# Tokens, memory tokens and norm weights laid out transposed by the host, with a tile shared in SBUF and other TensorE costs in a planner

## The chip, the cores and the metric

The kernel runs on one core of a Trainium2 chip. The metric is the device time of one execution in microseconds; three executions of the kernel before gave 803.38, 802.14 and 803.23 us, a median of 803.23 us. One further execution was recorded by the profiler, and every row below comes from it.

## What is computed

Two decoder layers over 256 tokens of width 1024 in float32. Each layer is a token mixer, a cross-attention into 256 memory tokens and a SwiGLU block, each behind an RMS norm and added to the residual stream `x`. Cut to what the change touches:

```python
h = rms_norm(x, norm_mix[i])            # x / sqrt(mean(x*x) + eps) * gain
if i % 2 == 0: x = x + dsa_moba_mixer(h, ...)      # token indexer, top 64 keys, two head groups
else:          x = x + nsa_mixer(h, ...)           # compressed, selected and window branches
q = rms_norm((rms_norm(x, norm_mem[i]) @ w_q), q_norm)
k, v = split(rms_norm(mem, norm_mem_src[i]) @ w_kv)
x = x + (softmax(q @ rms_norm(k, k_norm).T * scale) @ v) @ w_o
x = x + swiglu(rms_norm(x, norm_ffn[i]), w_in, w_out)
```

## The kernel before, in words

**Products.** Every float32 operand of a big product is split into a rounded half and a remainder (`hi`, `lo`), and each product is three matmuls (`mm3`): hi·hi, hi·lo, lo·hi. A product needs its tokens with the model dimension on the partitions. So the norm (`norm`, line 619) transposes `x` on TensorE, four 128x128 blocks per half row block, and `evac_gain` (line 608) multiplies by the norm's weights on DVE into `gv`, rounds that into the tile `h` (hi) and subtracts for the other half (lo). The scale 1/rms of a token is applied later, after the product, from sums of squares that ACT makes of the untransposed `x` (the tile `junk` takes the squares, accumulated into `ss`).

**Weights.** `plan_block` lists all weight blocks of 2x128x512 in the order of use. `load` (line 374) brings one by SP's queue into one of 3 buffers `raw`; `pusher` (line 395) makes its hi half (ACT or DVE) and its lo half (DVE) in one of 6 buffers `whl`, frees `raw` and issues the next load. `gemm` (line 571) walks the blocks for one tile of 128 tokens, 12 matmuls for a block of 512 columns; 1024 rows are four blocks.

**Order.** All work is written as generators. `Steps.run` (line 84) picks, one instruction at a time, the ready operation that an estimate of the engines' clocks (`Est`, line 140, with the costs of `cost`, line 236) lets start first. The order in which instructions stand on each engine is thus fixed when the program is built, from estimated costs; on the chip each engine takes its instructions in that order and waits with semaphores. Almost every instruction is recorded at one line (L232), so rows are told apart by tiles.

**Names.** In layer 0 the first product (`s`, 424 columns: `mm` with 128x424) feeds the small heads and the indexer; then follow `aq`, `bk`, `bq`, `bv`. `di`, `dk` and `t` are evacuated pieces that TensorE transposes (into `tp`), `ikT` the indexer's keys, `sp` scores, `acc` the indexer's sum, from which `top` (line 839) takes the best 64 keys, `sn` the softmax, `pt` its transpose, `po` the values' product. `mem_prep` (line 1242, spawned after `bq` in layer 0 and after the last query product in layer 1) loads the memory tokens (512 KB per 128 tokens), squares, transposes and splits them into buffers `slab`; `mem_k` (line 1267) then runs the product `mk`, which starts for a tile of 128 tokens when all 1024 dimensions of that tile are there. Line 448 on holds the start: the first loads of `x`, of the weights, and of `rows`, the norm weights as 76 rows of 128, which one TensorE transpose turns into `gT`.

Of the kernel before, what the change touches and what calls it, by code (L numbers as in the profile page):

```python
# [15 lines left out]
P = 128  # L16
D = 1024
# [122 lines left out]
class Est:  # L140


    def __init__(self, nc):
        self.clk = {"PE": 0.0, "V": 0.0, "S": 0.0, "G": 0.0, "D": 0.0, "port": 0.0}
        self.wr, self.rd, self.busy = {}, {}, {}
        self.now = 0.0
        self.eng = {n: Est.Engine(self, n, e) for n, e in
                    (("PE", nc.tensor), ("V", nc.vector), ("S", nc.scalar), ("G", nc.gpsimd))}
# [45 lines left out]
    def issue(self, e, outs, ins, cost):  # L194
        lock = self.locks(e, outs, ins)
        t = max(self.clk[e], self.after(e, outs, ins), self.clk["port"] if lock else 0.0)
        if e == "PE":
# [6 lines left out]
            cost = c  # L204
        t += cost
# [8 lines left out]
    class Engine:  # L214
# [21 lines left out]
        def cost(self, name, a, k, outs, ins):  # L236
# [58 lines left out]
def trunk(ctx: ExitStack, tc: tile.TileContext, I, out):  # L295
# [59 lines left out]

    def load_x(t, h, at):
# [91 lines left out]
    load_x(0, 0, 3.5)  # L448
    nc.sync.dma_start(rows, I["gains"])
    est.note(rows, est.wr, 3.6, "D")  # L450
    load_x(0, 1, 4.4)
    clk["D"] = 3.3
    load(0, 1.1)
    load(1, 1.1)
    for h in range(2):
        clk["D"] += 0.73
        load_x(1, h, clk["D"] + 1.1)
    for i in range(2, RAWS):
        load(i, 1.1)
# [9 lines left out]
    gps, f = TP.take([P, 512])  # L469
    T.transpose(gps[:, :NG], rows, ident[:NG, :NG]).issue()  # L470
    gT = cp.tile([P, NG], F32, name="gT")
    V.tensor_copy(gT, gps[:, :NG]).issue()
    f()
# [12 lines left out]
    def tables():  # L486
# [21 lines left out]
        yield has(("mix0", 0), 2)  # L508
# [62 lines left out]
    def gemm(key, t, h, K, ev, need=None, part=None):  # L571
# [15 lines left out]

    def both(key, h, K, ev):
# [5 lines left out]
    junk = tp.tile([P, 512], F32, name="junk")  # L594
# [24 lines left out]
    def norm(key, t, col, ver):  # L619
# [10 lines left out]
        ss = tiny(2, "ss")  # L630
        for h in range(2):
            yield S.activation(junk, x[t][:, 512 * h:512 * h + 512], AF.Square, accum_out=ss[:, h:h + 1])
        vr[key, t] = yield from ms_root(ss, "h", 0, t)

# [115 lines left out]
    def mixer0():  # L750
# [3 lines left out]
        ikT = hp.tile([P, SEQ], F32R, name="ikT")  # L754
        av = hp.tile([P, NT, HD], F32, name="av")
# [83 lines left out]
        def top(t, nk, acc):  # L839
# [5 lines left out]
            b = hp.tile([P, SEQ], F32, name=f"bias{t}")  # L845
# [99 lines left out]
        for t in range(NT):  # L945
            yield from gemm((0, "s"), t, h[t], KD, ev_small, (("mix0", t), 0))
# [26 lines left out]
    def mixer1():  # L973
# [4 lines left out]
        kvT = hp.tile([P, G + 1, SEQ], F32, name="kvT")  # L978
# [250 lines left out]
        for t in range(NT):  # L1229
            yield from gemm((1, "kc"), t, h[t], KD, ev_kc, (("mix1", t), 0))  # L1230
# [11 lines left out]
    def mem_prep(L):  # L1242
        m = I["mem"][0].rearrange("(t p) d -> t p d", p=P)
        for t in range(NT):
            raw, rf = yield from T4.get([P, D])
            nc.sync.dma_start(raw, m[t])
            est.note(raw, est.wr, clk["PE"] + 6.0, "D")
            ss = tiny(2, "mss")
            for h in range(2):
                rs = raw[:, 512 * h:512 * h + 512]  # L1250
                yield S.activation(junk, rs, AF.Square, accum_out=ss[:, h:h + 1])
                hi = yield from SL.get([P, 4, P], F32R)
                lo = yield from SL.get([P, 4, P], F32R)
                ps, f = yield from TP.get([P, 512])
                for k in range(4):
                    yield T.transpose(ps[:, k * P:(k + 1) * P], rs[:, k * P:(k + 1) * P], ident)
                col = 32 + 8 * L + 4 * h
                yield from evac_gain(ps, f, hi[0], lo[0], gT[:, col:col + 4])
                mT[t, h] = (hi, lo)
            rf()  # L1260
            mvr[t] = yield from ms_root(ss, "m", L, t)
            done(("mT", L, t))

    def msel(t):
        return lambda k: tuple(mT[t, k // 4][e][0][:, k % 4, :] for e in range(2))
# [271 lines left out]
```

## Time and profile before

| | us |
|---|---|
| median of three executions | 803.23 |
| the profiled execution | 801.81 |
| its span, first to last instruction | 800.1 |
| TensorE matmul busy (PE) | 766.0 |
| TensorE weight load busy (PEld) | 632.1 |
| VectorE busy (DVE) | 537.5 |
| ScalarE busy (ACT) | 435.4 |

Of the rest, GpSimd (POOL) is busy for 130.9 us, and the DMA queues move 121.27 MB. PE leads by far; what is not in its busy time are 34 us in which it waits. The columns of a stretch tell how busy each engine is in it, with the number of instructions in brackets, then the granted TensorE clock as a share of full speed, the mean busy share of the 16 DMA engines and what they moved. Behind a row's bracket "idle before" stands the time that the engine had waited and what ended the wait. PEld overlaps PE.

### The profile page before, as it was taken

What the parts mean: (1) busy time and instruction counts of PE and PEld (TensorE: products, weight loads), DVE (VectorE), ACT (ScalarE), POOL (GpSimd) and SP (SyncE); (2) the same over time, 40 slices, a digit from 0 to 9 for tenths busy, and PEclk for the clock granted to TensorE, in tenths of its full rate; (3) what the DMA queues carried; (4) which work ended last, traced back from release to release, by engine and by line L of the source; (5) the groups of instructions that cost most, each with busy time, mean ns of one, the idle gap of its engine ahead of it and who ended that gap; (6) DMA issues with size and microseconds to landing.
All of it is one profiled execution on the core that took longest, in us unless ns stands there. A gap on an engine that the chain in (4) does not pass through costs nothing.

```text
span 800.1 us, 11833 instructions
## 1 busy us (share of the span) xinstructions
PE 766.0 (96%) x4259; PEld 632.1 (79%) x4259; DVE 537.5 (67%) x1096; ACT 435.4 (54%) x816; POOL 130.9 (16%) x192
## 2 busy tenths in 40 slices
PE   6878999999999999999999988999999999999998
PEld 5766777888888888888878776878897888889886
DVE  6779998877655655545727798887868565646541
ACT  5666887565544434444526788864656334435430
POOL 1544332110000000000007463230200000000000
PEclk9999999999999999999999999999999999999999
DMA  7613334635565553887315632033635656546761
GB/s 221 208 55 112 134 124 122 181 119 159 158 191 179 168 186 119 240 251 224 116 56 148 210 112 81 1 103 110 184 105 146 198 184 180 167 141 209 225 184 52
DMA packets 69482, 121.27 MB, mean 152 GB/s; under 512 B 8420, under 2 KB 15664, under 8 KB 69424
## 3 DMA queue, kind: packets, MB, share of 16 engines
q1 hardware_dynamic: 69392, 120.53, 49.2%
q8 instruction: 33, 0.54, 0.3%
q14 instruction: 25, 0.20, 0.1%
q0 software_dynamic: 32, 0.00, 0.0%
HBM read 119.46 MB, written 1.05 MB: 151 GB/s over the span
## 4 chain that ended last, share of the span: by engine, by line
PE 83%; DVE 7%; ACT 4%; DMA 2%; issue 2%; POOL 1%; SPq 0%; POOLq 0%; ACTq 0%; DVEq 0%
PE mm L232 61%; PE po L232 12%; PE tp L232 7%; PE sp L232 3%; DVE whl L232 2%; DMA raw<-in_ab_w_in 1%; DMA raw<-in_ffn_w_in 1%; ACT sn L232 1%; ACT whl L232 1%; DVE slab L232 1%; DVE acc L232 1%; ACT slab L232 1%; DVE sn L232 1%; DVE t L232 1%; POOL sn L232 1%
## 5 line engine op out<-in xcount | busy, mean ns | idle before, releaser
L232 PE MATMUL mm<-whl,h 128*128 128x512 f32 (+3 forms) x1776 | 397.8, 379 | 8.5 <-DVE whl L232 6.9
L232 PEld LDWEIGHTS mm<-whl,h 128*128 128x128 f32 x1776 | 310.8, 189 | 68.0 <-DVE whl L232 8.9
L232 DVE TENSOR_TENSOR whl<-raw,whl 128x1024 fp32r<-128x1024 f32 (+3 forms) x232 | 270.9, 1170 | 116.6 <-ACT whl L232 112.4
L232 ACT ACTIVATE whl<-raw 128x1024 fp32r<-128x1024 f32 (+3 forms) x211 | 213.2, 1014 | 160.1 <-DMA raw<-in_ffn_w_in 38.4
L232 PE MATMUL mm<-whl,slab 128*128 128x512 f32 (+1 forms) x840 | 200.2, 376 | 0.9 <-DVE x L232 0.8
L232 PEld LDWEIGHTS mm<-whl,slab 128*128 128x128 f32 x840 | 140.6, 189 | 27.7 <-issue 2.4
L232 PE MATMUL po<-whl,slab 128*128 128x512 f32 x264 | 68.4, 396 | 0.0
L232 ACT ACTIVATE slab<-tp 128x256 fp32r<-128x256 f32 (+2 forms) x63 | 28.3, 471 | 56.3 <-PE tp L232 55.9
L232 PEld LDWEIGHTS po<-whl,slab 128*128 128x128 f32 x264 | 49.4, 188 | 11.4
L232 POOL TENSOR_TENSOR rh<-vh,mhalf 128x1 f32<-128x1 f32 x12 | 9.5, 794 | 293.6 <-DVE vh L232 283.1
L232 ACT ACTIVATE sn<-sn,mx 128x128 f32<-128x128 f32 (+1 forms) x96 | 42.7, 447 | 6.9 <-DVE mx L232 6.5
L232 PE MATMUL tp<-ident,t 128*128 128x128 f32 x224 | 34.8, 277 | 2.7 <-DVE slab L232 2.3
L232 PE MATMUL tp<-ident,sn 128*128 128x128 f32 (+1 forms) x180 | 30.9, 281 | 4.8 <-POOL sn L232 3.8
L232 DVE TENSOR_TENSOR x<-mm,x 128x512 f32<-128x512 f32 x36 | 24.6, 687 | 16.0 <-PE mm L232 15.9
L232 PEld LDWEIGHTS tp<-ident,t 128*128 128x128 f32 x224 | 27.1, 142 | 9.6 <-DVE slab L232 2.8
L232 ACT ACTIVATE pt<-tp 128x512 f32<-128x512 f32 (+2 forms) x51 | 27.0, 536 | 13.7 <-PE tp L232 11.8
L232 DVE CUSTOM_DVE_ANT_0 sn<-sp,cm,rq 128x128 f32<-128x128 f32 (+1 forms) x80 | 30.5, 410 | 4.9 <-PE sp L232 3.8
L232 POOL TENSOR_TENSOR sn<-sn,rc 128x512 f32<-128x512 f32 (+2 forms) x27 | 25.5, 944 | 43.5 <-DVE rc L232 28.6
L232 ACT ACTIVATE t<-mm,rh 128x512 f32<-128x512 f32 (+1 forms) x26 | 17.0, 654 | 27.0 <-PE mm L232 27.0
L232 PEld LDWEIGHTS tp<-ident,sn 128*128 128x128 f32 (+1 forms) x180 | 20.7, 141 | 11.6 <-POOL sn L232 5.2
L232 ACT ACTIVATE t<-mm 128x512 f32<-128x512 f32 (+2 forms) x46 | 23.7, 553 | 10.0 <-PE mm L232 8.0
L232 DVE SCALAR_TENSOR_TENSOR t<-mm,rh,t 128x512 f32<-128x512 f32 (+1 forms) x24 | 16.9, 704 | 18.2 <-PE mm L232 18.2
(200 smaller groups left out, 676.3 us busy)
## 6 DMA issues: line engine op xcount, KB each, us to landing
raw<-in_ffn_w_in SPq DMA_DIRECT2D x80, 512.0 KB, 3.8
raw<-in_ffn_w_out SPq DMA_DIRECT2D x44, 512.0 KB, 4.5
raw<-in_ab_w_in SPq DMA_DIRECT2D x16, 512.0 KB, 3.9
raw<-in_mem_w_kv SPq DMA_DIRECT2D x16, 512.0 KB, 4.0
raw<-in_nsa_w_in SPq DMA_DIRECT2D x16, 512.0 KB, 3.7
raw<-in_ab_w_out SPq DMA_DIRECT2D x8, 512.0 KB, 3.6
raw<-in_mem_w_q SPq DMA_DIRECT2D x8, 512.0 KB, 4.2
raw<-in_mem_w_o SPq DMA_DIRECT2D x8, 512.0 KB, 3.6
```

Source lines behind the costliest of these rows:

```text
L232: return f(*a, **{q: v() if q in ("start", "stop") and callable(v) else v for q, v in k.items()})
```

## The change

The host adds three arrays: `x_t` and `mem_t` (128 partitions x 8 x 256 tokens: the tokens transposed) and `gains_t` (128 x 76). `gT` is loaded and not transposed. For the first norm, four loads of 256 KB bring `x_t` into `slab` buffers, and `norm0` makes hi (rounded product with the weight of the partition) and lo from each 128x128 block; the rows of `x` are loaded behind them, for the sums of squares and the residual. `mem_prep` does the same with `mem_t`, two times 128 dimensions at a time for all 256 tokens, in both layers, and `mk` may begin with the first pair of dimensions. `mem_root` loads the rows of `mem` as well, in layer 0 alone, and its roots serve both layers. `junk` is gone (squares go to a free `t2` buffer), and the indexer's `acc` and `bias` live in a tile that layer 1's `kvT` takes over (`tag="kvT"`). In the planner, a switch between outputs of up to 64 partitions and more costs 0.09 us, a matmul at a column position 0.012 instead of 0.053, and a rounded one n x 0.00043 + 0.009 instead of n x 0.000422.

```diff
@@ Est.issue
+            thin = outs[0].shape[0] <= 64
+            if thin != self.thin:
+                t += 0.09
+            self.thin = thin
@@ Est.Engine.cost
                 if k.get("tile_position", (0, 0))[1]:
-                    return 0.053
+                    return 0.012
                 if ins[0].dtype == F32R:
-                    return n * (1 if n >= 256 else 4) * 0.000422
+                    return n * 0.00043 + 0.009
@@ trunk, the start
-    load_x(0, 0, 3.5)
+    nc.sync.dma_start(gT, I["gains_t"])
+    xfirst = []
+    for i in range(NB):
+        r, f = SL.take([P, 2, SEQ])
+        nc.sync.dma_start(r, I["x_t"][:, 2 * i:2 * i + 2])
...
+        xfirst.append((r, f))
+        if i < RAWS:
+            load(i, 1.1)
     nc.sync.dma_start(rows, I["gains"])
...
-    T.transpose(gps[:, :NG], rows, ident[:NG, :NG]).issue()
-    V.tensor_copy(gT, gps[:, :NG]).issue()
+    def gained(src, gain, hi, lo):
+        yield move(hi, src, gain)
+        yield V.scalar_tensor_tensor(lo, src, gain, hi.bitcast(F32), op0=OP.mult, op1=OP.subtract)
+    def norm0():
+        for b in range(NB):
+            r, f = xfirst[b]
+            for j in range(2):
+                k = 2 * b + j
+                for t in range(NT):
+                    yield from gained(r[:, j, t * P:(t + 1) * P], gT[:, k:k + 1], hT[t][0][:, k], hT[t][1][:, k])
+            f()
+            done("mix0")
...
@@ index
-                acc = hp.tile([P, SEQ], F32, name="acc", tag="acc", bufs=2)
+                acc = rowsT[:, t, :]
@@ mem_prep
-            raw, rf = yield from T4.get([P, D])
-            nc.sync.dma_start(raw, m[t])
+            raw, rf = yield from T2.get([P, 2, SEQ])
+            nc.sync.dma_start(raw, I["mem_t"][:, 2 * b:2 * b + 2])
...
-                for k in range(4):
-                    yield T.transpose(ps[:, k * P:(k + 1) * P], rs[:, k * P:(k + 1) * P], ident)
-                yield from evac_gain(ps, f, hi[0], lo[0], gT[:, col:col + 4])
+                yield from gained(raw[:, j], gT[:, c:c + 1], hi[0][:, j], lo[0][:, j])
...
-            yield has(("mT", L, t))
-            yield from gemm((L, "mk"), t, msel(t), KD, ev)
+            yield from gemm((L, "mk"), t, msel(t), KD, ev, pairs(("mT", L)))
```

Because the planner decides the order, work moves in both attention stretches. Three places:

SP's queue at the start of the program, before (`raw` are weight blocks):

```order
L358 DMA x_72<-in_x 128x512
L449 DMA rows<-in_gains 76x128
L358 DMA x_72<-in_x 128x512
L381 DMA raw_79<-in_ab_w_in 128x2x424
L381 DMA raw_81<-in_ab_w_in 128x2x424
L358 DMA x_73<-in_x 128x512 x2
L381 DMA raw_85<-in_ab_w_in 128x2x424
L381 DMA raw_159<-in_ab_w_in 128x2x424
```

and with the change:

```order
L457 DMA gT<-in_gains_t 128x76
L462 DMA slab_78<-in_x_t 128x512
L389 DMA raw_80<-in_ab_w_in 128x2x424
L462 DMA slab_82<-in_x_t 128x512
L389 DMA raw_84<-in_ab_w_in 128x2x424
L462 DMA slab_86<-in_x_t 128x512
L389 DMA raw_88<-in_ab_w_in 128x2x424
L462 DMA slab_90<-in_x_t 128x512
L468 DMA rows<-in_gains 76x128
L366 DMA x_72<-in_x 128x512 x2
L366 DMA x_73<-in_x 128x512 x2
L389 DMA raw_157<-in_ab_w_in 128x2x424
```

The first weight block moves ahead of half of the tokens, and the fourth now stands behind all of the transposed and all of the plain tokens.

TensorE in layer 0, before, at the end of the first tile of `bk` (`mm_444`), where the indexer's pieces are transposed and its scores made:

```order
L232 MATMUL mm_444<-whl_422,h_112 128x512
L232 MATMUL tp_509<-ident,di 128x128
L232 MATMUL tp_513<-ident,t_431 128x128 x4
L232 MATMUL tp_527<-ident,t_431 128x128 x4
L232 MATMUL tp_530<-ident,t_469 128x128 x4
L232 MATMUL sp_544<-ikT,slab_512 128x256 x2
L232 MATMUL tp_556<-ident,t_469 128x128 x4
L232 MATMUL sp_566<-ikT,slab_512 128x256 x2
L232 MATMUL tp_572<-ident,dk 128x128
L232 MATMUL sp_584<-ikT,slab_526 128x256 x2
L232 MATMUL tp_581<-identr,t_542 128x128 x4
L232 MATMUL tp_598<-identr,t_542 128x128 x2
```

and with the change, where the first of these stand in the two tiles of `aq` (`mm_361`, `mm_434`), one product earlier:

```order
L238 MATMUL mm_361<-whl_342,h_117 128x512 x2
L238 MATMUL mm_361<-whl_342,h_118 128x512
L238 MATMUL mm_361<-whl_342,h_117 128x512 x2
L238 MATMUL tp_425<-ident,t_330 128x128 x4
L238 MATMUL mm_361<-whl_342,h_118 128x512
L238 MATMUL mm_434<-whl_286,h_119 128x512
L238 MATMUL tp_439<-ident,di 128x128
L238 MATMUL mm_434<-whl_286,h_119 128x512
L238 MATMUL mm_434<-whl_286,h_120 128x512
L238 MATMUL mm_434<-whl_286,h_119 128x512 x2
L238 MATMUL mm_434<-whl_286,h_120 128x512
L238 MATMUL tp_449<-ident,t_330 128x128 x4
```

The block of transposes and scores without a product among them is gone; each piece has three or more matmuls of `aq` or `bk` around it.

TensorE in layer 1's attention, before, where the first matmuls of `mk` (`mm_5134`) stand, ahead of them scores, transposes and values' products only:

```order
L232 MATMUL po_4755<-pt_5056,vv 64x128 x4
L232 MATMUL tp_5096<-ident,sn_5009 128x128 x4
L232 MATMUL sp_5091<-slab_4145,slab_4721 128x256
L232 MATMUL sp_5091<-slab_4149,slab_4721 128x256
L232 MATMUL sp_5091<-slab_4145,slab_4721 128x256
L232 MATMUL sp_5091<-slab_4149,slab_4721 128x256
L232 MATMUL sp_5114<-kbd,slab_4584 128x30 x3
L232 MATMUL po_4755<-pt_5097,vv 64x128 x4
L232 MATMUL sp_5114<-kbd,slab_4584 128x30
L232 MATMUL mm_5134<-whl_4476,slab_4999 128x512 x2
L232 MATMUL mm_5134<-whl_4476,slab_5000 128x512
```

and with the change (`mk` is `mm_4866`):

```order
L238 MATMUL po_4565<-pt_4853,vv 64x128 x4
L238 MATMUL po_4751<-pt_4881,vv 64x128 x4
L238 MATMUL tp_4933<-ident,sn_4851 128x128 x4
L238 MATMUL sp_4915<-slab_4125,slab_4662 128x256
L238 MATMUL sp_4915<-slab_4129,slab_4662 128x256
L238 MATMUL sp_4915<-slab_4125,slab_4662 128x256
L238 MATMUL sp_4915<-slab_4129,slab_4662 128x256
L238 MATMUL po_4751<-pt_4934,vv 64x128 x4
L238 MATMUL tp_4959<-ident,sn_4902 128x128 x4
L238 MATMUL mm_4866<-whl_4452,slab_4869 128x512 x2
L238 MATMUL sp_4956<-slab_4126,slab_4684 128x256
L238 MATMUL sp_4956<-slab_4130,slab_4684 128x256
```

The first of them now stand among the second attention tile's scores (`slab_4126`), before they stood at the third's (`slab_4145`).

## Rows read from the trace of the kernel before

**Rows 1.** The page, part 1: busy time, share of the span, instructions.

```profile
PE 766.0 (96%) x4259; PEld 632.1 (79%) x4259; DVE 537.5 (67%) x1096; ACT 435.4 (54%) x816; POOL 130.9 (16%) x192
```

**Rows 2.** Busy time by stretch; last three: granted clock, DMA share, GB/s.

```profile
0.00:8.20 8.20, 2.30 (x9) 1.57 (x10) 1.77 (x12) 1.91 (x2) 1.84 (x10) 1.00 0.66 205
8.20:16.30 8.10, 6.85 (x27) 5.50 (x27) 8.10 (x18) 4.89 (x9) 0.95 (x1) 1.00 0.75 215
...
42.00:50.80 8.80, 4.35 (x30) 3.59 (x29) 7.46 (x19) 5.07 (x11) 1.32 (x7) 0.94 0.23 70
50.80:53.00 2.20, 2.20 (x9) 1.67 (x8) 1.18 (x6) 2.06 (x5) 1.81 (x3) 0.50 0.00 0
53.00:82.00 29.00, 25.17 (x130) 19.86 (x129) 26.27 (x70) 18.31 (x33) 15.20 (x23) 1.00 0.30 91
82.00:100.00 18.00, 16.80 (x103) 13.22 (x102) 16.00 (x56) 14.69 (x36) 7.51 (x11) 1.00 0.38 128
100.00:160.00 60.00, 59.88 (x362) 46.96 (x361) 51.93 (x132) 43.39 (x102) 16.21 (x16) 1.00 0.47 142
...
456.00:500.00 44.00, 38.35 (x318) 31.86 (x316) 38.27 (x141) 36.69 (x110) 24.97 (x29) 0.96 0.33 110
```

**Rows 3.** The same view, two short stretches of the start.

```profile
4.00:6.00 2.00, 1.05 (x5) 0.65 (x4) 1.05 (x10) 0.18 (x1) 0.00 (x0) 1.00 0.65 172
6.00:8.00 2.00, 1.09 (x4) 0.72 (x4) 0.52 (x2) 0.45 (x1) 0.00 (x0) 1.00 1.00 364
```

**Rows 4.** Instructions in order of time, the start: start us, us, engine.

```profile
10.11 3.13 PE L232 MATMUL mm<-whl,h 128*128 128x424 f32 x10
...
16.31 8.64 PE L232 MATMUL mm<-whl,h 128*128 128x424 f32 x41 [0.19 <-DVE whl L232]
```

**Rows 5.** The chain that ended last, 24 to 42 us: start us, us, what.

```profile
27.44 12.60 PE mm L232 x55
```

**Rows 6.** TensorE in order of time, 42 to 52 us.

```profile
43.64 1.09 PE L232 MATMUL tp<-ident,t 128*128 128x128 f32 x8 [1.58 <-DVE slab L232]
...
49.12 0.51 PE L232 MATMUL tp<-identr,t 128*128 128x128 f32 x4 [1.04 <-DVE slab L232]
...
50.86 1.61 PE L232 MATMUL mm<-whl,h 128*128 128x512 f32 x3
```

**Rows 7.** Weight loads by shape, 60 to 104 us: busy us, mean ns.

```profile
L232 PEld LDWEIGHTS sp<-slab,slab 128*128 128x128 f32 x28 | 4.0, 189 | 0.5
L232 PEld LDWEIGHTS tp<-ident,t 128*128 128x128 f32 x32 | 3.8, 140 | 1.7 <-issue 1.0
```

**Rows 8.** Groups by shape over the span: busy us, mean ns, idle before.

```profile
L232 DVE TENSOR_TENSOR gv<-tp,gT 128x512 f32<-128x512 f32 x32 | 22.0, 687 | 6.8 <-PE tp L232 6.7
...
L232 DVE SCALAR_TENSOR_TENSOR slab<-tp,kv,slab 128x128 fp32r<-128x128 f32 x18 | 5.2, 344 | 0.9 <-ACT slab L232 0.7
...
L232 DVE SCALAR_TENSOR_TENSOR slab<-tp,kv,slab 128x256 fp32r<-128x256 f32 x8 | 3.6, 475 | 1.1 <-ACT slab L232 1.1
```

**Rows 9.** The same view, ACT.

```profile
L232 ACT ACTIVATE junk<-x 128x512 f32<-128x512 f32 x24 | 15.0, 624 | 0.4
...
L232 ACT ACT_TABLE_LOAD x6 | 7.7, 1283 | 0.9 <-PEq L1527 0.8
L232 ACT ACTIVATE slab<-tp,kv 128x128 fp32r<-128x128 f32 x18 | 5.3, 368 | 0.4 <-PE tp L232 0.4
...
L232 ACT ACTIVATE whl<-raw 128x848 fp32r<-128x848 f32 x3 | 2.7, 908 | 2.3 <-DMA raw<-in_ab_w_in 2.2
```

**Rows 10.** TensorE in order of time, 480 to 502 us: `mem` transposes, first `mk`.

```profile
491.79 0.60 PE L232 MATMUL tp<-ident,t 128*128 128x128 f32 x4
...
499.97 0.95 PE L232 MATMUL mm<-whl,slab 128*128 128x512 f32 x3
```

**Rows 11.** Waits of SP's queue; DMA issues of the memory tokens: landing us.

```profile
SPq L1246 <- PE tp L232: 4.0, 2, 2.5
...
t<-in_mem SPq DMA_DIRECT2D x4, 512.0 KB, 4.2
```

More of the change, by code (lines that the diff above doesn't have):

```diff
@@ L16 @@
 P = 128
+NB = 4
 D = 1024
@@ L145, in __init__ @@
         self.wr, self.rd, self.busy = {}, {}, {}
+        self.thin = False
         self.now = 0.0
@@ L354, in trunk @@
     posi = cp.tile([P, NT], I32, name="posi")
+    gT = cp.tile([P, NG], F32, name="gT")
     def load_x(t, h, at):
@@ L446, in setup @@
         return ident
-    load_x(0, 0, 3.5)
-    nc.sync.dma_start(rows, I["gains"])
[L450 to L459, printed above, removed]
+    clk["D"] = 1.4
+    nc.sync.dma_start(gT, I["gains_t"])
+    est.note(gT, est.wr, 3.4, "D")
+    xfirst = []
+    for i in range(NB):
+        r, f = SL.take([P, 2, SEQ])
+        nc.sync.dma_start(r, I["x_t"][:, 2 * i:2 * i + 2])
+        clk["D"] += 1.2
+        est.note(r, est.wr, clk["D"] + 1.1, "D")
+        xfirst.append((r, f))
+        if i < RAWS:
+            load(i, 1.1)
+    nc.sync.dma_start(rows, I["gains"])
+    est.note(rows, est.wr, clk["D"] + 1.1, "D")
+    for t in range(NT):
+        for h in range(2):
+            clk["D"] += 1.2
+            load_x(t, h, clk["D"] + 1.1)
     ident = setup()
@@ L507, in tables @@
         yield S.activation(cos, ang, AF.Sin)
-        yield has(("mix0", 0), 2)
+        yield has("mix0", NB)
         nsin = cp.tile([P, NT, HALF], F32, name="nsin")
@@ L577, in gemm @@
             u = yield from unit(plan_at[key] + k0 // 2)
-            if need and k0 % 4 == 0:
-                yield has(need[0], need[1] + 1 + k0 // 4)
+            if need:
+                yield need(k0)
             for j in range(2):
@@ L586, in gemm, with halves, pairs @@
         spawn(ev(ps[:, :n], free, t))
+    def halves(key):
+        return lambda k0: has(key, 1 + k0 // 4)
+    def pairs(key):
+        return lambda k0: has(key, 1 + k0 // 2)
     def both(key, h, K, ev):
@@ L754, in mixer0 @@
         ikT = hp.tile([P, SEQ], F32R, name="ikT")
+        rowsT = hp.tile([P, G + 1, SEQ], F32, name="kvT", tag="kvT")
         av = hp.tile([P, NT, HD], F32, name="av")
@@ L945, in mixer0 @@
         for t in range(NT):
-            yield from gemm((0, "s"), t, h[t], KD, ev_small, (("mix0", t), 0))
+            yield from gemm((0, "s"), t, h[t], KD, ev_small, pairs("mix0"))
         yield from both((0, "aq"), h, KD, ev_q(0, "aqT"))
@@ L1229, in mixer1 @@
         for t in range(NT):
-            yield from gemm((1, "kc"), t, h[t], KD, ev_kc, (("mix1", t), 0))
+            yield from gemm((1, "kc"), t, h[t], KD, ev_kc, halves(("mix1", t)))
         yield from both((1, "ks"), h, KD, ev_sw(0))
@@ L1274, in ev @@
             rk = tiny(MH, "mrk")
+            yield has("mr", 1 + t)
             yield from inv_rms(ps, MH, MD, mvr[t][0], 1.0 / MD, 1.0, rk)
@@ L1358, in mem_attn @@
         for t in range(NT):
-            yield from gemm((L, "mq"), t, hsel(t), KD, ev_q, ((("mem", L), t), 0))
+            yield from gemm((L, "mq"), t, hsel(t), KD, ev_q, halves((("mem", L), t)))
         for p in range(2):
@@ L1362, in mem_attn @@
                 yield from gemm((L, "mv"), t, msel(t), KD, ev_v(p), part=(256 * p, 256))
-        for t in range(NT):
-            for h in range(2):
-                for e in range(2):
-                    mT[t, h][e][1]()
+        for b in range(NB):
+            for e in range(2):
+                mT[b][e][1]()
         for p in range(2):
@@ L1427, in ffn @@
             for t in range(NT):
-                yield from gemm((L, "g", j), t, hsel(t), KD, ev_g, ((("ffn", L), t), 0))
+                yield from gemm((L, "g", j), t, hsel(t), KD, ev_g, halves((("ffn", L), t)))
             for t in range(NT):
@@ L1475, in trunk @@
     spawn(tables(), 3)
-    for t in range(NT):
-        spawn(norm("mix0", t, 0, 1))
+    spawn(norm0())
     spawn(pusher(), haste)
@@ L1515, in layout @@
     a = {n: np.ascontiguousarray(inputs[n]) for n in _INS}
+    for n in ("x", "mem"):
+        a[n + "_t"] = np.ascontiguousarray(np.asarray(inputs[n])[0].reshape(SEQ, KD, P).transpose(2, 1, 0))
     a["gains"] = np.concatenate([np.asarray(inputs[n]).reshape(-1, P) for n in NORMS] +
```

51 lines of the change are left out of this document (33 added, 18 removed).

## The prediction

> **What bounds the kernel now.** Read the totals first: PE is busy for 766.0 of 800.1 us [rows 1], so what there is to win are its 34 us of waiting and the work that is taken off it. Then the stretches [rows 2], to see where these lie. PE is busy for 2.30 of the first 8.20 us and 6.85 of the next 8.10: it waits for data. From 42.0 to 50.8 us it is busy for 4.35 of 8.80, and from 50.8 to 53.0 the granted clock is 0.50, the lower of its two levels (1.2 GHz). Between 53 and 100 us it misses 5.0 us, from 100 to 160 only 0.12 of 60, and from 456 to 500 5.65 us. Then who ends the waits: in the hole at 42 to 50.8 each of the four long waits, of which two are shown, was ended by DVE [rows 6]. There a chain transposes, evacuates and scores, and PE has no product in its order to fill the time. A gain must come from such holes or from PE's own work where it is full; what is saved on DVE or DMA counts only through these.
>
> **The sum, against the profiled execution (801.8 us; the median of three runs is 803.2, 1.4 above it).**
>
> *The start.* Its 17 transposes go, and count for nothing: they stand where PE idles for 5.9 of 8.2 us [rows 2]. If that cover were gone, 17 x 0.14 us [rows 7] = 2.4 us. The weights set the pace instead. Up to the fourth weight block SP now issues 4 x 256 KB transposed and 4 x 256 KB plain tokens, twice 38 KB of norm weights and 4 x 424 KB: 3.9 MB. Before, 205 GB/s for 8.2 us were 1.7 MB [rows 2]. The other 2.2 MB take 6.1 us at the best rate of the start, 364 GB/s [rows 3], 10.3 us at the 215 GB/s of the second stretch [rows 2], and 12.9 us at 172 [rows 3]: the block is there at 14.3, 18.5 or 21.1 us. ACT is not free earlier than that either. From about 4.2 us it does 14 roundings at 0.37 (128x128), three of the weights at 0.91, four squares at 0.62, each with some 0.2 to read the sum (my allowance), a table load of 1.28 [rows 9] and two sines: 13.1 us, so 17.3. With the block at 17.5, 0.91 on ACT and 1.03 on DVE (its size at the same rate as ACT's, a little slower) make it ready at 19.5, while before PE went on with it at 16.31 [rows 4]. But then 41 matmuls were left up to 25 us; now 18 of the 24 of the first tile are done when it comes. Left are 30 at 0.20 us (8.64 us for 29 of them and 12 of 512 columns [rows 4]), so 25.5. Before, PE stood still again until 27.44, then ran at 12.60/55 = 0.229 us each [rows 5]. To the end of the first tile of `bk` it then had 60 matmuls, 41.2 us; now 72 from 25.5, 42.0 us. **+0.8 us.** Bounds: +0.2 if the block lands at 14.3, +3.4 if at 21.1. If weights for `aq` came late too, they'd be hidden: they need be there 2.75 us apart, and 0.5 MB at 215 GB/s takes 2.4.
>
> *The hole at 42 to 50.8 us.* Between the last product of `bk`'s first tile, about 41.3 us, and the next at 50.86 [rows 6] PE does 27 transposes at 0.14 and 8 score matmuls at 0.19 [rows 7], 5.3 us in 9.5. Now the order puts products between them, so 4.2 us of waiting can go, and with the hole the slow clock: about 3.3 us at half speed [rows 2] did work worth 1.6. At most -5.8, at worst 0, if the wait moves along. I take **-4.5**, nearer the first: every piece has products around it, but PE takes its rows in order and the chain's other half, on ACT and DVE, remains. What is late next is DVE, which is busy for 26.3 of 29 us from 53 on [rows 2].
>
> *The memory tokens' 32 transposes.* At 0.14 us each [rows 7] they are 4.5 us of PE. Layer 0's 16 lie where PE is 93% busy: -2.3. Of layer 1's, the first eight start at 491.8 and 494.8, between waits [rows 10]; the later eight lie in a full stretch: -1.1. **-3.4**, bounds 0 and -4.5. The matmul row says that PE is full there. The Trainium skill (Perfetto Trace Analysis, Identifying the Most-Contended Engine) calls that row a bad measure, and the weight loads' share a good one. By that share, 46.96 of 60 us [rows 2], a fifth would be free, and this term would be 0; I stay with the row, since dense matmuls run at 0.229 us for 512 columns in the higher clock level [rows 5].
>
> *`mk` in layer 1 starts earlier.* Its first matmul was at 499.97 [rows 10], since all of a tile had to be loaded, transposed, weighted and split. It now starts by pairs of dimensions, one attention tile earlier, and fills waits. 456 to 500 misses 5.65 us [rows 2]; only the last third of it can be filled. **-1.5**, bounds 0 and -3.5.
>
> *Nothing on the path.* DVE loses 12 weightings at 0.69 and ten lo halves of the same size (15.1 us), gains 16 lo halves at 0.34 and 16 at 0.48 (13.1) [rows 8], and is below PE in every stretch from 82 us on [rows 2]. The 2 MB more of loads are some 9 us at 215 GB/s while DMA is busy for a third or so of the time [rows 2]; if it were not, 9 us at most. The shared tile frees space only; its next use comes 300 us later. The squares' borrowed buffer is released after one step; if none were free, ACT would wait a step of 0.6 us. The planner's costs change the order alone; outside the two attention stretches the order stays nearly word for word: 0, and up to 3 either way from reshuffled waits, 53 to 100 us above all.
>
> Sum: +0.8 - 4.5 - 3.4 - 1.5 = -8.6 us: 793.2 for the profiled execution, **794.6** beside the median of 803.2. About 0.2%, 1.6 us, is what a measurement of this kernel can tell from no change.
>
> **Rivals.**
> *The hole moves along.* PE's order is strict: if ACT, which has more to do at the start, is late with the pieces, the products between the transposes wait as well. For it: ACT is the co-bound at 17.3 us. Against: pieces and products are far apart. Without that term: 799.1. With the worst start too, 801.7.
> *PE is not full.* Then the 32 transposes are worth nothing: 798.0. Against it stands 59.88 busy of 60 us.
> *A cold start.* In the first stretch ten matmuls of 424 columns took 3.13 us, 0.31 each, against 0.20 later [rows 4], though the granted clock shows 1.00 (the higher level) throughout. If the removed transposes had brought PE up to speed, the 30 matmuls after the fourth block would cost 0.10 more each: 3.0 us, 797.6. The Trainium skill (TensorE: Matmul & The Clock Gate, Part 1) says that the slow clock is the default and sustained work releases it; by that the delay is real. Its Part 4 says that transposes don't count for it, which speaks against this rival. Against it also: 18 matmuls run before the 30.
> *More than the hole.* If the wait for weights at 53 to 82 us, 3.8 us [rows 2], goes too, since DVE is asked earlier: 790.8.
> *Slower: `mk` is fed late.* Memory tokens now come in pairs by eight loads, each of 4.2 us to land at twice the size [rows 11], into buffers that evacuated products also use; the issue can block SP's queue, as it did for 2.0 us each twice [rows 11], with weights behind it. PE's order mixes `mk` with the attention, so that a pair that is late stops both. From 1.1 us per pair on average the 8.6 us are gone; at half a landing, 2.1 us, it is +16.8, 811; at 1.5 us 806.6. For: all eight pairs have this form. Against: four buffers take turns, and three raw and six finished weight blocks stand ready. That the change does nothing can't be: the transposes are gone from the order.
>
> **How the numbers follow.** The forecast as summed, 790 to 799 with its bounds: 0.53. The hole moves along 0.14; PE not full 0.08; cold start 0.07; more than the hole 0.08; `mk` late 0.10. Faster by over 0.2% (below 801.6) holds the forecast, the three weaker gains but for a part of the first (0.04, with the worst start) and the greater gain, 0.86, and 0.85 with a little of the forecast's own tail taken off; within 0.2% 0.06; slower 0.09. The range 788 to 801 leaves out the late `mk` (0.10), the worst part of the first rival (0.04) and the lower end of the greater gain (0.04), near 2 in 10.
>
> **What would show it.** The first matmul before 8.22 us, the last weight of `s` ready near 19.5 us and `bk`'s first tile done near 42; no stretch of several us with PE half busy between 40 and 55 us and no granted 0.50 there; the second tile of `bk` begun about 4 us earlier than 50.86; PE's busy time lower by 5 to 7 us, weight loads fewer by 49; the first `mk` matmul of layer 1 about 10 us before the third attention tile's scores end. Wrong it would be if PE waits for `h` or the fourth weight block beyond 21 us, if a wait as long as the hole stands at the evacuated pieces, or if PE waits at `mk` for slabs and SP's queue for `t` buffers.

## The result and the profile after

The changed kernel takes 807.76 us (median of four, 807.48 to 808.26), the kernel before in the same session 802.93 us: ratio 1.0059, 95% interval 1.0046 to 1.0071. It is **slower by 4.8 us** where 8.6 us less were forecast. The profiled execution has a span of 806.6 us.

The busy totals of the page after, which answer to [rows 1]:

```profile
PE 765.7 (95%) x4210; PEld 631.3 (78%) x4210; DVE 536.2 (66%) x1100; ACT 435.0 (54%) x827; POOL 124.9 (15%) x190
```

The 49 transposes are gone, yet PE's busy time stayed at 766 us. The stretches after (columns as in [rows 2]):

```profile
8.20:16.30 8.10, 7.32 (x18) 5.29 (x18) 7.81 (x28) 7.55 (x20) 0.00 (x0) 1.00 1.04 360
16.30:25.00 8.70, 4.60 (x13) 3.95 (x14) 6.97 (x37) 4.67 (x11) 2.90 (x6) 0.65 0.39 107
42.00:50.80 8.80, 8.80 (x48) 7.22 (x47) 8.64 (x19) 6.19 (x12) 7.10 (x13) 1.00 0.46 127
53.00:82.00 29.00, 27.46 (x139) 21.75 (x138) 25.76 (x64) 20.42 (x37) 15.67 (x18) 1.00 0.48 149
82.00:100.00 18.00, 12.20 (x72) 8.69 (x70) 17.73 (x59) 13.14 (x34) 7.99 (x11) 0.93 0.47 154
100.00:120.00 20.00, 16.80 (x114) 13.29 (x114) 16.10 (x65) 14.44 (x46) 4.16 (x6) 0.81 0.28 88
120.00:160.00 40.00, 39.95 (x227) 31.73 (x227) 33.65 (x68) 24.69 (x50) 6.20 (x6) 1.00 0.36 120
456.00:500.00 44.00, 40.30 (x299) 33.13 (x298) 38.40 (x123) 35.09 (x94) 23.29 (x31) 1.00 0.48 153
```

The hole at 42 to 50.8 us is gone: PE is busy for all of it, at the full clock, where it was busy for 4.35 us [rows 2]. A new hole stands at 82 to 120 us. To see where time was won and lost, I count the product matmuls (those that read `whl`) through: both kernels have 2880 in the same order, so the k-th does the same work in both. Their start times in the profiled executions (us):

| k | what begins | before | after | after - before |
|---|---|---|---|---|
| 40 | `s`, second tile | 20.48 | 27.45 | +7.0 |
| 96 | `bk`, first tile | 35.53 | 43.96 | +8.4 |
| 120 | `bk`, second tile | 50.86 | 50.71 | -0.1 |
| 240 | `mk` of layer 0 | 95.70 | 87.09 | **-8.6** |
| 264 | `mk`, second tile | 105.3 | 117.2 | **+11.8** |
| 400 | past layer 0's mixer | 156.2 | 161.3 | +5.1 |
| 1520 | just inside layer 1's mixer | 424.3 | 429.3 | +5.0 |
| 2040 | layer 1's SwiGLU | 608.2 | 614.2 | +6.0 |

So the products ran 8.6 us ahead at the start of `mk` (that this is the size forecast for the end is chance), and within its first tile they lost 20. PE's rows there, from its timeline after:

```profile
93.40 1.64 PE L238 MATMUL mm<-whl,slab 128*128 128x512 f32 x6
94.97 0.44 PE L238 MATMUL po<-pt,av 128*64 128x128 f32 x4
97.10 0.48 PE L238 MATMUL tp<-ident,sn 128*128 128x128 f32 x2 [1.69 <-POOL sn L238]
102.15 0.69 PE L238 MATMUL po<-pt,av 128*64 128x128 f32 x4 [4.57 <-ACT pt L238]
102.77 1.65 PE L238 MATMUL mm<-whl,slab 128*128 128x512 f32 x3
```

From 95.4 to 102.15 us PE does two transposes. It waits for softmax pieces, and no `mk` matmul (`mm<-whl,slab`) stands between. The timeline names ACT; ACT's own timeline tells why the piece was late:

```profile
97.16 1.06 ACT L238 ACTIVATE whl<-raw 128x1024 fp32r<-128x1024 f32 x1 [0.55 <-DMA raw<-in_ab_w_out]
99.76 1.06 ACT L238 ACTIVATE whl<-raw 128x1024 fp32r<-128x1024 f32 x1 [1.54 <-DMA raw<-in_ab_w_out]
...
101.74 0.36 ACT L238 ACTIVATE pt<-tp 128x256 f32<-128x256 f32 x1
```

ACT did weights of the output projection, asked for early because the products were ahead, and waited for their DMA with `pt` behind. But why had PE nothing else? SP's timeline shows when the memory tokens (`in_mem_t`) were asked for:

```profile
68.15 0.34 SPq L1303 DMA_DIRECT2D t<-in_mem_t  x1
...
81.14 0.34 SPq L1303 DMA_DIRECT2D t<-in_mem_t  x1
...
93.27 0.46 SPq L1303 DMA_DIRECT2D t<-in_mem_t  x1
...
102.51 0.47 SPq L1303 DMA_DIRECT2D t<-in_mem_t  x1
```

One pair of dimensions every 9 to 13 us. `mem_prep` is a loop: it loads a pair, splits it on ACT and DVE, and only then asks for the next. The third pair's halves were ready at 103, the fourth's at 111.7, and the first tile of `mk` needs all four. Before, it needed the two halves of one row block, which one load brought.

The series is one of the plan, not of the chip alone. The planner reckons 6 us for each landing (`clk["PE"] + 6.0` in the code), and it places a pair's splits on ACT and DVE, and the next load on SP, behind that. Layer 1 of the same kernel shows that the loads themselves need not be late: SP asked for all four pairs within 4 us, and the remainders on DVE still started over 24 us (SP's timeline, then the view of the tile `slab`: ns of the shortest, median and longest, then the first and the last start):

```profile
489.00 0.42 SPq L1303 DMA_DIRECT2D t<-in_mem_t  x1
...
491.93 1.41 SPq L1303 DMA_DIRECT2D t<-in_mem_t  x3
...
L238 DVE SCALAR_TENSOR_TENSOR slab<-t,gT,slab x8: 476/483/612, 495.8 to 519.6; 128x256 fp32r<-128x256 f32 x8
```

The four pairs were finished there at 496.8, 504.6, 512.4 and 520.0, 7.8 us apart. No run changed the 6.0: that it sets this spacing is read from the code, not tested.

### The profile page after: what moved, and what is told of

It is laid out like the page before. It is cut to its first block, busy times and chain, and to the rows that moved or that the text cites. A ratio compares the mean times of both kernels' runs of the same rounds, so it can differ in the third digit from the quotient of the medians.

```text
span 806.6 us, 11778 instructions
## 1 busy us (share of the span) xinstructions
PE 765.7 (95%) x4210; PEld 631.3 (78%) x4210; DVE 536.2 (66%) x1100; ACT 435.0 (54%) x827; POOL 124.9 (15%) x190
## 4 chain that ended last, share of the span: by engine, by line
PE 81%; DVE 9%; ACT 4%; DMA 3%; issue 2%; POOL 1%; SPq 0%; DVEq 0%; ACTq 0%; POOLq 0%
PE mm L238 60%; PE po L238 11%; PE tp L238 7%; PE sp L238 3%; DVE whl L238 3%; ACT whl L238 2%; DVE sn L238 2%; DMA raw<-in_ffn_w_out 1%; DMA raw<-in_ffn_w_in 1%; DVE t L238 1%; DVE slab L238 1%; ACT t L238 1%; ACT sn L238 1%; DMA raw<-in_ab_w_out 1%; ACT slab L238 1%
## 5 line engine op out<-in xcount | busy, mean ns | idle before, releaser
L238 PE MATMUL mm<-whl,h 128*128 128x512 f32 (+3 forms) x1776 | 402.5, 382 | 15.5 <-ACT whl L238 8.3
L238 PEld LDWEIGHTS mm<-whl,h 128*128 128x128 f32 x1776 | 315.7, 192 | 75.2 <-DVE whl L238 9.1
L238 PEld LDWEIGHTS mm<-whl,slab 128*128 128x128 f32 x840 | 142.6, 189 | 31.5 <-issue 2.4
L238 ACT ACTIVATE slab<-tp 128x256 fp32r<-128x256 f32 (+2 forms) x72 | 31.0, 462 | 48.3 <-PE tp L238 48.1
L238 PE MATMUL tp<-ident,t 128*128 128x128 f32 x192 | 30.0, 277 | 1.5 <-DVE t L238 0.8
L238 PEld LDWEIGHTS tp<-ident,t 128*128 128x128 f32 x192 | 23.3, 142 | 7.7 <-DVE t L238 2.5
L238 PE MATMUL sp<-slab,slab 128*128 128x256 f32 x160 | 27.5, 299 | 0.0
```

The source lines that it names most:

```text
L238: return f(*a, **{q: v() if q in ("start", "stop") and callable(v) else v for q, v in k.items()})
```

## Experiments

All ratios are to the kernel before on the same chip, with 95% intervals.

### Which part?

The change has three parts that can be had apart: the costs (C), the start with `x_t` and `gains_t` (S), the memory tokens (M). A fourth, the shared tile with the borrowed buffer for the squares, stays in every run but only_costs, so its worth is not separated. Each edit is taken from the change or undone in it; of the longer two the telling lines:

```diff
 costs undone
-                    return 0.012
+                    return 0.053
-                    return n * 0.00043 + 0.009
+                    return n * (1 if n >= 256 else 4) * 0.000422
-                t += 0.09
+                t += 0.0
 start undone
...
-    spawn(norm0())
+    for t in range(NT):
+        spawn(norm("mix0", t, 0, 1))
...
 memory tokens undone
...
-            nc.sync.dma_start(raw, I["mem_t"][:, 2 * b:2 * b + 2])
+            nc.sync.dma_start(raw, m[t])
...
-            yield from gemm((L, "mk"), t, msel(t), KD, ev, pairs(("mT", L)))
+            yield has(("mT", L, t))
+            yield from gemm((L, "mk"), t, msel(t), KD, ev)
```

only_costs: 

> The kernel before with the planner's new TensorE costs alone (802.9 us before, 807.8 with the whole change). Theory, the DVE queue: the loss comes from the second tile's top-64 search, which ended at 103.8 us in place of 98.1, because the order puts more remainders of weight blocks (1.21 us each) ahead of its last step on DVE: 26 in place of 21. Here 23 stand ahead, so the search ends about 2 to 3 us later and the time is 803 to 806. Rival, the costs alone: the new costs make the whole loss, 807 to 812. Rival, memory pairs or start: no change, 802 to 804.

only_start: 

> The transposed first tokens and norm weights alone, with the old costs and the old way of the memory tokens. DVE queue: 23 remainders ahead of the last step of the search, 803 to 806. Rival, the start's late fourth weight block (product 40 came 7 us later): the whole loss, 807 to 810. Rival, costs or memory pairs: 801 to 804.

only_memory: 

> The transposed memory tokens alone, with the old costs and the old start. DVE queue: 20 remainders ahead of the last step of the search, one fewer than before, so nothing is lost there and the 32 transposes are saved: 796 to 801. Rival, memory pairs fed late (loads and splits among the search's steps): the whole loss, 806 to 810.

start_and_memory: 

> The whole change but with the planner's old TensorE costs. Rival, the parts add: the start gave -3.1 us and the memory tokens +2.3 by themselves, so 801 to 802. Theory, the loss is one meeting of waits that the order of the whole change alone makes (ScalarE waits for weight blocks at 97 to 100 us with a piece of the attention behind it): another order, another result, and without that meeting the start's gain stays: 797 to 801.

costs_and_start: 

> The whole change but with the old way of the memory tokens. The parts add: the costs gave 0 and the start -3.1, so 799. Theory, one meeting of waits: the weights of the output projection are asked for as early as with the whole change if the products run ahead as far; 799 to 806. If the new costs together with the new start make the loss, 806 or more.

costs_and_memory: 

> The whole change but with the old start. The parts add: 0 and +2.3, so 804.4. Theory, one meeting of waits: not before the start's products run ahead, so 801 to 806 and no wait of several us at the softmax piece near 100 us.

| | us | ratio | without M |
|---|---|---|---|
| only_costs | 802.21 | 1.0001 [0.9987, 1.0015] | |
| only_start | 799.01 | 0.9961 [0.9947, 0.9976] | |
| costs_and_start | 799.71 | 0.9972 [0.9962, 0.9983] | |
| only_memory | 804.43 | 1.0030 [1.0019, 1.0042] | 1 |
| costs_and_memory | 805.26 | 1.0044 [1.0029, 1.0058] | 1.0001 |
| start_and_memory | 803.44 | 1.0025 [1.0016, 1.0035] | 0.9961 |
| all three | 807.76 | 1.0059 [1.0046, 1.0071] | 0.9972 |

In each of the four pairs the memory part costs: 2.4, 3.4, 5.1 and 7.0 us (ratio less the one without it, times 802). The start gains 3 us alone. An edit changes the planned order of the whole kernel, so each of these runs is another order, and the pattern over the four pairs carries the reading, not one run. My first theory, weight remainders ahead of the last step of the top-64 search on DVE, missed all three first runs. In only_memory the search ended at 94.3 us, earlier than before (98.1), and the kernel was slower; in only_start it ended later, at 103.6, and the kernel was faster. The second theory, one meeting of waits at 97 to 100 us that another order avoids, missed with start_and_memory: 803.44 us where it gave 797 to 801.

### The search

```diff
-                yield V.max(m8, acc[:, :nk])
-                yield V.match_replace(acc[:, :nk], m8, acc[:, :nk], TAKEN)
+                yield same(V.max(m8, acc[:, :nk]), lambda m8=m8: nc.vector.max(m8, acc[:, :32]))
+                yield same(V.match_replace(acc[:, :nk], m8, acc[:, :nk], TAKEN),
+                           lambda m8=m8: nc.vector.match_replace(acc[:, :32], m8, acc[:, :32], TAKEN))
```

(`same` issues the second instruction with the planner's record of the first, so that the order stays.) 

> The whole change in its own order, word for word, but the 16 steps of the top-64 search on DVE look at 32 columns in place of 128 or 256 (the picked keys are no longer the best 64; this part of the computation is changed). That takes some 7 us off DVE between 58 and 104 us. Theory, DVE decides the stretch (weight buffers come free late behind the search): the wait of 4.6 us at 97.6 and the waits around it go, 800 to 804. Rival, the waits there are of DMA and ScalarE alone: less than 1 us, 806.5 to 808.

Measured: 806.86 us, 1.0061 [1.0046, 1.0076]. One of its windows:

```profile
82.00:100.00 18.00, 11.71 (x70) 8.32 (x68) 14.24 (x55) 12.67 (x32) 7.10 (x11) 0.94 0.47 155
```

and PE's largest wait between 82 and 120 us (us in total, times, longest):

```profile
PE po L238 <- ACT pt L238: 5.3, 2, 4.9
```

DVE is busy for 14.24 us of this stretch in place of 17.73, and PE waits as long as before. The wait was 5.0 us in all and 4.6 at the longest in the change. DVE's load does not make the hole in this order.

### The form of the memory tokens, their buffers

by_row_block: blocks of 128 tokens and half of the dimensions, as before, but without transposes.

```diff
+        for t in range(NT):
+            for h in range(2):
+                raw, rf = yield from T2.get([P, 512])
+                nc.sync.dma_start(raw.rearrange("p (a b) -> p a b", a=4), I["mem_t"][:, 4 * h:4 * h + 4, t * P:(t + 1) * P])
...
+                yield from evac_gain(raw, rf, hi[0], lo[0], gT[:, c:c + 4])
+                done(("mT", L, t))
```

> The whole change, but the transposed memory tokens come by row block and half of the dimensions (128 x 4 x 128), as the plain ones did before, and mk waits by such halves; no transposes. Theory, mk is fed late: by pairs of dimensions the first tile of mk needs all four parts, and they came over 30 us (its 24 matmuls took 87.1 to 116.9 us, before 95.7 to 105.1). By row block it needs two of four: its 24 matmuls take about 10 us, and the time is 796 to 800 (costs and start alone gave 799.7). Rival, the missing transposes or the second set of loads make the loss: 804 to 808.

by_row_block_old_costs: 

> The same with the planner's old costs. Theory, mk is fed late: 795 to 800 (the start alone gave 799.0). Rival, the missing transposes or the second set of loads: 802 to 805, as with the pairs (803.4).

roots_behind (`spawn(mem_root())` moved from the head of `mem_prep` to its end): 

> The whole change, but the plain rows of the memory tokens (four loads into the same four buffers as the pairs) are asked for behind the four pairs in place of beside them. If the buffers are what makes the pairs late, the pairs come sooner and mk's first tile ends near 105 us: 801 to 805. If it is the pairs' own form (each needs two free buffers, a step on ScalarE and one on DVE among the attention's), little changes: 806 to 809.

own_buffers (`MR`, three buffers of its own):

```diff
+    MR = Slots(est, tp, "mr", 3)
-            raw, rf = yield from T2.get([P, 2, SEQ])
+            raw, rf = yield from MR.get([P, 2, SEQ])
```

> The whole change, but the pairs are loaded into three buffers of their own, not into those that the evacuated products use. If these buffers make the pairs late: three pairs are there by 75 us, mk's first tile runs from 87 us on with few breaks, fills the hole of 4.6 us at 97.6, 799 to 804. If ScalarE and DVE, which split the pairs, are what they wait for: 805 to 809.

Measured: 805.93 us, 1.0052 [1.0036, 1.0069]; 803.32, 1.0014 [1.0004, 1.0023]; 809.94, 1.0100 [1.0085, 1.0115]; 806.14, 1.0054 [1.0031, 1.0077]. All four times missed what my theory, or the better case of the buffers, gave: both by_row_block runs lie where missing transposes or the second set of loads were to blame, own_buffers where ACT and DVE were, and roots_behind above both of its ranges. In by_row_block `mk`'s first tile did as I expected: its 24 matmuls took 87.1 to 98.7 us. Then the second tile had no tokens. SP's timeline of by_row_block:

```profile
68.30 0.37 SPq L1304 DMA_DIRECT2D t<-in_mem_t  x1
...
79.18 0.37 SPq L1304 DMA_DIRECT2D t<-in_mem_t  x1
...
92.74 0.47 SPq L1304 DMA_DIRECT2D t<-in_mem_t  x1
...
100.33 0.37 SPq L1304 DMA_DIRECT2D t<-in_mem_t  x1
```

and the remainders of the four parts on DVE, from the view of the tile `slab` (ns of the shortest, median and longest, then the first and the last start):

```profile
L238 DVE TENSOR_TENSOR slab<-gv,slab x4: 679/683/693, 81.1 to 116.4; 128x512 fp32r<-128x512 f32 x4
```

The last part is split at 116.4 us. The loads come at nearly the same four times whatever the form, and with own buffers too (63, 80, 93, 101). So it is neither the form nor the buffers; what these runs share is the loop, in which a part's turn comes in the plan only when the one before is split. On the chip SP does not wait for that split: with own buffers it asked for the second pair at 80.55 us, right behind a weight load, and the first pair was split only at 85.2. roots_behind asks for the plain rows at 105 to 133 us. Why it is worse than the change is not shown: at the first matmul of `mk`'s second tile it is already 14.5 us behind the kernel before, where the change is 11.8.

### The loads ahead of the splitting, and a late feed where there was none

loads_ahead, with the buffers `MR` as above:

```diff
+        for b in range(3):
+            fetch()
         for b in range(NB):
-            raw, rf = yield from T2.get([P, 2, SEQ])
-            nc.sync.dma_start(raw, I["mem_t"][:, 2 * b:2 * b + 2])
-            est.note(raw, est.wr, clk["PE"] + 6.0, "D")
+            raw, rf = got[b]
...
             rf()
+            if len(got) < NB:
+                fetch()
```

> The whole change, but the first three pairs of the memory tokens are loaded at once into three buffers of their own, ahead of the splitting of the first (as changed, a pair is loaded only when the one before it is split: 68, 81, 93 and 103 us). Theory, mk is fed late by these four round trips: the pairs are split by 95 us, mk ends before 110 us in place of 128, and the time is 798 to 803. Rival, the saved transposes are no gain since DVE and ScalarE are the bound around mk, whatever the feeding: 805 to 809.

loads_ahead_old_costs: 

> The same with the planner's old costs (the whole change with old costs was 803.4, the start alone 799.0). Theory, four round trips: 796 to 800. Rival: 802 to 805.

spawned_earlier, and start_fed_late (on only_start, moved behind `bv`):

```diff
 spawned_earlier
+        spawn(mem_prep(0), 2)
         yield from both((0, "bq"), h, KD, ev_q(1, "bqT"))
-        spawn(mem_prep(0), 2)
 start_fed_late
-        spawn(mem_prep(0), 2)
         yield from both((0, "bv"), h, KD, ev_v)
+        spawn(mem_prep(0), 2)
```

> The whole change with the preparation of layer 0's memory tokens started one product earlier, ahead of bq in place of behind it. Theory, mk is fed late: all four round trips begin some 10 us sooner, mk's last pair is there near 100 us, 800 to 804. Rival, DVE and ScalarE are the bound: their work for the pairs only stands earlier and delays the indexer instead, 805 to 810.

> The suspected cost put on a kernel without it: the transposed start alone (799.0, memory tokens as before, transposes and all), but layer 0's memory tokens are asked for one product later, behind bv. Theory, mk is fed late: as with the whole change, products that could fill the attention's waits are missing between 95 and 110 us, 803 to 810. Rival: the feeding doesn't matter, 798 to 800.

Measured: loads_ahead 799.04 us, **0.9953** [0.9934, 0.9972]; with the old costs 796.86 us, **0.9935** [0.9920, 0.9950]; spawned_earlier 801.36, 0.9985 [0.9974, 0.9997]; start_fed_late 807.02, **1.0063** [1.0046, 1.0080]. All four lie in the range that the theory gave. loads_ahead has neither the transposes nor fewer loads than by_row_block, so the two rivals of by_row_block are not the loss. SP's timeline of loads_ahead_old_costs:

```profile
63.04 1.41 SPq L1307 DMA_DIRECT2D mr<-in_mem_t  x3
...
79.09 0.34 SPq L1307 DMA_DIRECT2D mr<-in_mem_t  x1
```

and two of its windows:

```profile
82.00:100.00 18.00, 16.65 (x96) 12.32 (x96) 16.92 (x58) 15.46 (x39) 5.64 (x9) 1.00 0.34 122
100.00:120.00 20.00, 20.00 (x134) 16.28 (x133) 18.46 (x63) 15.21 (x43) 8.53 (x9) 1.00 0.45 153
```

SP's timeline of start_fed_late:

```profile
91.22 0.54 SPq L1287 DMA_DIRECT2D t<-in_mem  x1
...
109.70 0.46 SPq L1287 DMA_DIRECT2D t<-in_mem  x1
```

and the same two windows of it:

```profile
82.00:100.00 18.00, 15.46 (x104) 12.02 (x102) 16.63 (x65) 15.68 (x43) 5.39 (x9) 1.00 0.44 130
100.00:120.00 20.00, 18.73 (x133) 14.31 (x132) 16.47 (x63) 16.25 (x53) 6.72 (x8) 0.91 0.35 122
```

With three loads issued within 1.4 us the hole is gone: PE is busy for 36.7 of the 38 us, as before the change. With a late load a hole of the same kind, though smaller (34.2 of 38, only_start has 36.9), appears in a kernel that has the transposes and no pairs at all. When `mk`'s matmuls of layer 0 started, from PE's rows (us), and the ratio:

| | first | 24th | 48th | ratio |
|---|---|---|---|---|
| before | 95.7 | 105.1 | 118.1 | 1 |
| only_start | 94.8 | 103.4 | 111.6 | 0.9961 |
| start_fed_late | 109.2 | 123.2 | 132.4 | 1.0063 |
| the whole change | 87.1 | 116.9 | 129.1 | 1.0059 |
| by_row_block | 87.1 | 98.7 | 128.1 | 1.0052 |
| own_buffers | 89.7 | 107.9 | 125.6 | 1.0054 |
| spawned_earlier | 90.6 | 101.9 | 116.7 | 0.9985 |
| loads_ahead | 89.4 | 100.7 | 109.7 | 0.9953 |
| loads_ahead_old_costs | 91.3 | 101.2 | 110.7 | 0.9935 |
| only_memory | 96.6 | 114.0 | 125.7 | 1.0030 |
| costs_and_memory | 93.3 | 107.2 | 118.3 | 1.0044 |
| by_row_block_old_costs | 90.8 | 100.6 | 113.7 | 1.0014 |

Runs with the 48th by 112 us are faster than before, those with it after 125 us are slower. It isn't the whole account: costs_and_memory ends `mk` as before and loses 3.5 us, and by_row_block_old_costs ends it 4.4 us earlier and gains nothing. What they lose elsewhere was not followed up.

### Is it the feed alone, and is more feed better?

memory_ahead_alone is loads_ahead with the old start and the old costs; ahead_and_earlier is loads_ahead_old_costs with the move of spawned_earlier.

> Only the transposed memory tokens (old start, old costs), with three loads ahead as in loads_ahead. With one load at a time it was 804.4 (before: 802.1). Theory, four round trips: the late feed is gone and part of the 32 transposes' 4.5 us is seen, 797 to 801. Rival, the saved transposes are no gain by themselves and the 796.9 of loads_ahead_old_costs is luck of that order: 801 to 804.

> loads_ahead_old_costs (796.9) with the preparation also started ahead of bq. Theory: once mk's first tile has its tokens when it asks for them, at about 90 us, earlier is worth nothing more: 795 to 799. Rival, feeding is still short: 792 to 795. If the earlier splits hold up the indexer: 799 to 803.

Measured: 799.54 us, 0.9968 [0.9956, 0.9980]; 803.29 us, 1.0014 [1.0004, 1.0024]. The first stands against 1.0030 with one load at a time: 5 us for the feed, in a third order. Its forecast, 797 to 801, held. The second came out at 803.29, against 795 to 799 by the theory and just above the 799 to 803 that I gave to earlier splits in the way: counted by product matmuls, it is 1.7 us ahead of before at the second tile of `bk`'s end (k = 144) and 6.3 behind at `bv` (k = 192), and PE's longest wait there, 4.5 us, is for an evacuated product. That these splits are what held it up is argued, not shown.

The best kernel of the study is loads_ahead_old_costs, 796.86 us, 5.4 us faster than before (802.24 in its session) and, by the two ratios, some 10 faster than the change.

## Why the prediction was wrong, point by point

**The step that failed** is "Nothing on the path", where the prediction puts the new loads of the memory tokens at 0 ("while DMA is busy for a third or so of the time"). It priced the loads by their bytes and the splits by their DVE time, and never by their round trips. Four parts stand in a row, each with a landing of 3.0 to 5.5 us that the plan reckons at 6, and with its splits behind other work on ACT and DVE: 34 us from the first load to the last in layer 0. With these loads the memory part, forecast at -3.4 - 1.5, gave +7.0 on top of the other two (1.0059 against 0.9972). In the profiled executions all of that stands ahead of layer 1: at k = 1520 the kernel without the memory part is 4.9 us ahead of before, the whole change 5.0 behind.

With the loads ahead, the same part gives -1.5 on the other two (0.9953 against 0.9972, their intervals overlap) and -2.6 alone (memory_ahead_alone, 0.9968, clear of 1). So "the memory tokens' 32 transposes, -3.4" was too large as well: memory_ahead_alone is 0.5 us ahead past layer 0's mixer (k = 400), where layer 0's sixteen were to give -2.3. That term was also missummed, since sixteen at 0.14 us are 2.24, and 93% of that is 2.1.

**The rival that held it** was "`mk` is fed late", at 0.10, with 806.6 to 811 against 807.8 measured. That the pairs are late and stop the attention with them was right. The rest of it was not, and the number is in good part luck: it charged all eight pairs alike, while the loss stands at layer 0's four, and it blamed the shared buffers, while own buffers left 1.0054. Its place in the profile was wrong too: I looked for PE waiting at `mk` for slabs. The planner reckoned that the pairs would be late and put attention pieces there instead; so the long waits are recorded at `po` and `tp`, with ACT and POOL as releasers, and none of them names the memory tokens. What was missing was a filler.

**PE is full**, "59.88 busy of 60 us", was read as a property of the stretch. It was one of the order: `mk` filled the attention's waits. Without it, 82 to 120 us has 29.0 us of busy PE (12.20 + 16.80) in 38, where it had 16.80 of 18 to 100 us and, past that, missed 0.12 of 60 [rows 2].

**The start** was mis-sized, +0.8 with a bound of +3.4: the first tile of `bk` began 8.4 us later. ACT came to the fourth block at 17.45 us (forecast 17.3), but its remainder was made on DVE at 20.25 us, behind the steps for the rotation tables (DVE's timeline):

```profile
18.30 0.28 DVE L238 COPY growt<-tp 128x112 f32<-128x112 f32 x1 [0.63 <-PE tp L238]
...
20.25 1.00 DVE L238 TENSOR_TENSOR whl<-raw,whl 128x848 fp32r<-128x848 f32 x1
```

Those tables wait for a transpose on PE, whose timeline reads:

```profile
17.82 0.45 PE L238 MATMUL tp<-slab,one 76*128 76x112 f32 x2 [1.82 <-DVE slab L238]
18.40 0.46 PE L238 MATMUL mm<-whl,h 128*128 128x424 f32 x1
21.30 11.30 PE L238 MATMUL mm<-whl,h 128*128 128x424 f32 x44 [2.44 <-DVE whl L238]
```

PE had stood still for most of 16.0 to 21.3 us, and the next 44 matmuls, 29 of 424 columns and 15 of 512, took 11.30 us. By the rates of before it would have been some 9.3 (8.64 for 29 and 12 [rows 4], and three more at 0.229 [rows 5]). So some 2 us go with a slow clock, much like the cold start of a rival, yet not at the program's start but behind this wait (granted clock 0.65 from 16.3 to 25).

**The hole** was right in kind and also mis-sized, the other way: from the first to the second tile of `bk` went 15.3 us before and 6.75 now, 8.6 less where at most 5.8 were allowed. The two errors cancel: at the second tile of `bk` -0.1 us, forecast -3.7. only_start ends at -3.1, near the -3.7 of these two terms, but that is luck: in its profiled execution it is 0.6 us ahead at the second tile of `bk` and 1.1 behind at k = 400, and leads only past that (-1.8 at k = 1520). Where its gain comes from is open.

**Reshuffled waits**, "up to 3 either way, 53 to 100 us above all": the place was right, but the size was 20 us within one product tile. "What is late next is DVE" is not what the runs show: with 3.5 us less of DVE in that stretch nothing moved.

**Layer 1.** Between k = 1520 and 2040 the change loses 1.0 us where -2.6 was forecast; loads_ahead_old_costs gains 2.6 there (-2.8 to -5.4 against before), loads_ahead 2.0 and memory_ahead_alone 2.4. The size was right, for a kernel that loads ahead. In the change `mk`'s first matmul came 3.9 us earlier (496.1 us, before 499.97 [rows 10]), not 10, and the 24th of its first tile, with the pairs 7.8 us apart, only at 522.1, where before it came at 519.0.

**Open.** The costs give 0 alone. In the whole change and in by_row_block they lose 2.7 and 3.0 us (1.0059 against 1.0025, 1.0052 against 1.0014); with the start alone, with the memory part alone and with loads ahead it is some 1 us, not clear of noise. By which of the moved rows wasn't tried.

## What to carry to other kernels

Price a moved load by its round trips: who asks for it, after what, and how many stand in a row; bytes and busy shares say nothing of that. In a kernel whose order is planned, count them in the plan, with the landing that the plan assumes: it fixes where the users of the data stand, even if the data are there early. Cutting a transfer into finer pieces only starts its user earlier if the pieces are asked for ahead. And where a stretch is full because independent work fills a chain's waits, a change that delays the filler costs the waits, which the profile then books on the chain.

## What the runs showed of the hardware

The wait at 95 to 102 us cost more than itself. The granted clock in and behind it (windows of the change):

```profile
97.00:102.00 5.00, 0.48 (x2) 0.20 (x2) 4.57 (x8) 3.30 (x6) 0.05 (x1) 0.54 0.76 240
102.00:104.00 2.00, 1.85 (x7) 1.34 (x8) 1.94 (x9) 1.09 (x3) 0.38 (x1) 0.50 0.80 254
104.00:106.00 2.00, 2.00 (x10) 1.90 (x9) 0.99 (x4) 0.05 (x1) 0.93 (x2) 0.50 0.67 227
106.00:108.00 2.00, 2.00 (x8) 1.36 (x7) 1.93 (x9) 2.00 (x8) 0.00 (x0) 0.60 0.40 155
108.00:110.00 2.00, 1.35 (x11) 1.06 (x12) 2.00 (x9) 1.30 (x5) 1.04 (x1) 1.00 0.01 4
```

PE did two transposes in 6.7 us, fell to the lower level (1.2 GHz), and stayed there for some 5 us of work after; from 108 us it has 2.4 GHz again. By the granted shares, the 6 us to 108 did an estimated 2.8 us less than at the full clock (2 x 0.50 + 2 x 0.50 + 2 x 0.40). The Trainium skill (TensorE: Matmul & The Clock Gate, Part 1) says that the slow clock is the default and activity releases it; the rows agree. With the stretch behind the start's wait, this is likely part of why PE's busy total didn't fall with 49 instructions fewer; the sum was not closed.

The start's loads ran faster than I had assumed: 360 GB/s from 8.2 to 16.3 us with the 16 DMA engines busy throughout, where the same stretch before moved 215 [rows 2].
